# Hybrid attention layer on one core: weights' low parts between norm sums, and four subtractions on GpSimd

## The chip, the cores and the metric

The kernel runs on one core of a Trainium2 chip. The metric is the device time of one execution in microseconds, as the median of several executions. The engines are named as the profile names them: PE (TensorE's matrix multiplications), PEld (its weight loads), DVE (VectorE), ACT (ScalarE), POOL (GpSimd) and SP (SyncE, which here only issues DMAs).

## The reference

A layer with D = S = 1024, batch 1, depth 1, in float32. The input is normalised, multiplied by one wide weight matrix and split; differential softmax attention (8 heads) and gated linear attention (GLA, 4 heads) run on the parts; both are normalised, gated, joined, multiplied by `w_out`, normalised and added to the input.

```python
h = rms_norm(x, pre_g)                          # over D
z = einsum('bsd,de->bse', h, w_in)              # 1024 x 1024 x 7184
qa, ka, va, ga, qb, kb, vb, gb, gk_low = split_columns(z)
oa = diff_attention(qa, ka, va, lam)            # causal, two softmax maps a head
oa = rms_norm(oa, subln_g) * (1 - lam_init) * silu(ga)
log_a = log_sigmoid(gk_low @ w_gk_up + b_gk) / 16
ob = rms_norm(gla_chunked(qb, kb, vb, log_a), gla_g) * silu(gb)
x + rms_norm(concat([oa, ob]) @ w_out, post_g)
```

## The kernel before

**Products.** Each float32 operand of a large product is split into a high part, cast to the type that PE takes (ACT: `CAST`), and a low part, the operand less its high part (DVE: `TENSOR_TENSOR`). A product is three passes over PE: high by high, high by low, low by high. For `h @ w_in` both matrices are cut into 2 x 2 blocks and multiplied by a seven-product scheme (Strassen's, in Winograd's form): sums and differences of blocks are formed first, and seven products, numbered 1 to 7, take the place of eight. `LEFT` gives the left factor of each: `h11`, `h12`, `s4`, `h22`, `s1`, `s2`, `s3` for products 1 to 7.

**Steps.** `order` is a list of (column group, product). `go` walks it; `prepare` makes the weights of a step some steps ahead, `step` issues its matmuls. The first two column groups (`GATED`, the columns VB) come first, with products 1, 2, then 5, 6, 7, 4; `gated_weights(n)` makes their weights for both groups at once, two 128x1024 tiles `hi(0)`, `hi(1)` on ACT and two low parts `lo(0)`, `lo(1)` on DVE. For product 7 it leaves `lo` in the list `between`, from which the caller takes it.

**The first 80 us.** `norm_x` sums squares of a 128-row block of x (ACT), adds epsilon (DVE, `ssq`) and raises to -1/2 (POOL, `ssq`); `scale_x` multiplies the block's rows by it (DVE). `first(0)` and `first(1)` transpose rows 0 to 511 on PE (`xT`) and make `h11` and `h12` (`f1` keeps the unsplit `h12`); short `spin` products keep PE at work between the transposes. `blocks(j)` does so for rows 512 to 1023 (`t21`, `t22` and their sum `s1`); `differences(j)` makes s2 = t22 - (h11 - t21) in the tiles `s24` and splits it. Then follow `h22`, `s3` and, last, s4 = f1 - s2, which is written over s2 in `s24` by four DVE subtractions and then split.

**Product 6 to product 7.** Both add into the same PSUM banks, named x. Between them ACT copies a bank out (`COPY s<-x`), so the matmuls of product 7 of a column group may write only when the two copies of that group are done. Product 7 of the first group is the 24 matmuls that start near 66.5 us in the profile, that of the second the next 24.

**Order.** A scheduler orders the instructions of each engine's queue by a model of the time, within the dependences; instructions marked by `keep_in_program_order` (all while `pinned` holds) stay as written, and `tc.issue_after(i)` keeps what follows behind instruction i. Each engine then runs its queue strictly in that order, and waits on semaphores of the others.

**Helper lines.** Calls by way of `Queue` have line 66, matmuls line 144, transposes line 147; instructions are therefore told apart by their tiles. In names with buffer numbers (`s24_619`), the number is that of the tile.

Of the kernel before, what the change touches and what calls it, by code (L numbers as in the profile page):

```python
# [11 lines left out]
ALU = mybir.AluOpType  # L12
# [4 lines left out]
D = 1024  # L17
# [14 lines left out]
def hymba_kernel(  # L32
# [42 lines left out]
    act, dve, pool = Queue(nc.scalar), Queue(nc.vector), Queue(nc.gpsimd)  # L75

    def fp(t):
        return t.bitcast(F32)

    def cols(half):  # L80
        return slice(half * 512, half * 512 + 512)
# [239 lines left out]
    def gated_weights(n):  # L321

        name = {5: "b12"}.get(n)
        if name:
            load_gated(name)
        b11, b12, b21, b22, again = (
            gated_raws.get(name) for name in ("b11", "b12", "b21", "b22", "b21x")
        )
        src = {1: b11, 2: b21, 5: b11, 6: b11, 7: b12, 4: again, 3: b22}[n]
        a, b = {5: (b12, b11), 7: (b22, b12), 4: (again, b11)}.get(n, (None, None))  # L330
        own = {2: 1, 5: 1, 6: 3, 4: 1}.get(n)
        w = []
        for i in range(4):
            if i == own:
                w.append(kp.tile([P, 2, 512], F32R, tag="ks1", name="w"))
            elif n == 2 and i > 1:
                w.append(hw.tile([P, 2, 512], F32R, tag=f"h22_lo{i - 2}", name="w"))
            else:
                w.append(ap.tile([P, 2, 512], F32R, tag="ring", name="w", bufs=NRING))
        def hi(i):  # L340
            if a:
                dve.tensor_tensor(src[i], a[i], b[i], ALU.subtract)
            act.copy(w[i], src[i])

        def lo(i):
            lows[n] = dve.tensor_tensor(w[2 + i], src[i], fp(w[i]), ALU.subtract)

        if n == 1:
            for k in range(2):
                dve.tensor_copy(w[0][:, k], src[0][:, k])  # L350
            between[:] = [
                lambda: lo(1),
                lambda: (scale_x(3, cols(1)), lo(0)),
                lambda: act.copy(w[1][:, 1], src[1][:, 1]),
                lambda: (act.copy(w[1][:, 0], src[1][:, 0]), scale_x(2, cols(1))),
                lambda: [scale_x(st, cols(1)) for st in range(2)],
            ]
            return w[:2], w[2:]
        hi(0)
        if n == 7:  # L360
            hi(1)
            casts.append(act.latest)
            between.append(lo)
        else:
            hi(1)
            lo(0)
            lo(1)
        return w[:2], w[2:]

    between, lows = [], {}  # L370
# [181 lines left out]
    sums, key_stores, casts = {}, [], []  # L552
# [125 lines left out]
    def scale_x(st, cs):  # L678
        x_cs = xs[st][:, cs]
        return dve.tensor_scalar(x_cs, x_cs, norms[st], 1.0, ALU.mult, ALU.mult)  # L680
# [33 lines left out]
    for st in range(2):  # L714
        norm_x(st)
        scale_x(st, cols(0))
    norm_x(2)
    norm_x(3)
    scale_x(2, cols(0))
# [11 lines left out]
    f1 = hpool.tile([P, HB, 512], F32, tag="s4_lo0", name="f1")  # L731
# [26 lines left out]
    def parts(n, j, f, after=None):  # L758
        hi, lo = block(n)
        act.copy(at(hi, j), f)  # L760
        with tc.issue_after(after.ins) if after else nullcontext():
            return dve.tensor_tensor(at(lo, j), f, fp(at(hi, j)), ALU.subtract)
# [80 lines left out]
        prepare(i)  # L843
    first(0)
    norm_x(4, 5)
    for st in (4, 5):
        scale_x(st, slice(0, D))
    between.pop()()
    norm_x(6, 7)
    for st in (6, 7):  # L850
        scale_x(st, slice(0, D))
    hold[0] = 4
    for i in (2, 3):
        prepare(i)
# [14 lines left out]
    s24 = [kp.tile([P, 2, 512], F32, tag=f"k{i}", name="s24") for i in range(2)]  # L869
# [14 lines left out]
    for j in range(HB):  # L884
        s3_lo = parts("s3", j, t21[:, j], h22_lo)
# [5 lines left out]
    for i in range(2):  # L891
        for j in range(2 * i, 2 * i + 2):
            s = s24[i][:, j % 2]
            with tc.issue_after(s3_lo.ins):
                dve.tensor_tensor(s, f1[:, j], s, ALU.subtract)
        if not i:
            w_lo = between.pop()
            w_lo(0)
        for j in range(2 * i, 2 * i + 2):
            behind = [parts("s4", j, s24[i][:, j % 2], None if i else lows[7])]  # L900
        if not i:
            load_again(1)
            with tc.issue_after(behind[0].ins):
                w_lo(1)
# [365 lines left out]
    def parts_of(n):  # L1270
        return [(0, n)] if n <= 512 else [(0, 512), (512, n)]
# [27 lines left out]
    def scores(h, qb):  # L1299

        n = (qb + 1) * P
        qc = slice(qb % 4 * P, qb % 4 * P + P)
        st = const.tile([P, 6], F32, tag="stt", name="stt", bufs=4)
        if h == 0 and qb == NT - 1:
            for row, i in ((4, 7), (5, 6)):
                p1s[row] = pp.tile([P, (i + 1) * P], F32, tag=f"p0_{i}", name="p1", bufs=2)
        p0 = pp.tile([P, n], F32, tag=f"p0_{qb}", name="p0", bufs=1 + (qb > 5))
        if h == 0 and qb < 2:
            p1s[qb] = smp.tile([P, 512], F32, tag=("r", "fold")[qb], name="p1", bufs=1)
        p1 = p1s.pop(qb, None) or smp.tile([P, S], F32, tag="p1", name="p1", bufs=2)  # L1310
        for m, p in enumerate((p0, p1)):
            q = qk[h, "q", qb // 4][:, m, qc]
            parts = parts_of(n)
            if h == DA_HEADS - 1 and (qb, m) in ((1, 1), (0, 0), (0, 1)):

                parts = [(0, 512)]
            for i, (a, b) in enumerate(parts):
                sc = sc_bank("sc", [P, 512])
                for j, name in enumerate(("k", "ks")):
                    for half in range(2):  # L1320
                        lo, hi = max(a, half * 512), min(b, half * 512 + 512)
                        if lo < hi:
                            mm(
                                sc[:, lo - a : hi - a], q,
                                qk[h, name, half][:, m, lo - half * 512 : hi - half * 512],
                                start=(j == 0), stop=(j == 1),
                            )
                e = min(b, n)
                last = i == len(parts) - 1

                forced = (h, qb) == (0, NT - 2) or (h, qb, m) == (0, 3, 0)
                forced = forced or ((h, qb) == (0, 4) and m + i > 0)
                behind = tc.issue_after(lowest[0]) if forced else nullcontext()
                with behind:
                    ins = dve.tensor_tensor_reduce(
                        p[:, a:e], sc[:, : e - a],
                        maskt[:, NZ + P - (e - a) :] if last else maskt[:, : e - a],
                        1.0, 3e38 if i == 0 else st[:, 4 + m : 5 + m], ALU.add, ALU.min,
                        st[:, m : m + 1] if last else st[:, 4 + m : 5 + m],
                    )  # L1340
                if (h, qb) == (0, NT - 1):
                    lowest[:] = [ins.ins]
                c = 0.08 + (e - a) / 512 * 0.56
                if last:
                    act.activation(
                        p[:, :n], p[:, :n], AF.Exp, bias=st[:, m : m + 1], scale=-1.0,
                        accum_out=st[:, 2 + m : 3 + m],
                    )
                if last and m:
                    rec = dve.reciprocal(st[:, 4:6], st[:, 2:4])  # L1350
                    if h == 0 and qb in (4, 5):
                        lowest[:] = [rec.ins]
                    pool.tensor_scalar(
                        p1[:, :n], p1[:, :n], st[:, 5:6], lam, ALU.mult, ALU.mult
                    )
                    if qb != 5:
                        while mixed:
                            with tc.issue_after(ins.ins):
                                mixed.pop(0)()

                    def mix_maps():
                        dve.scalar_tensor_tensor(
                            p0[:, :n], p0[:, :n], st[:, 4:5], p1[:, :n], ALU.mult, ALU.subtract
                        )
                        w[h, qb] = p0

                    if h == 0 and qb > 2:
                        mixed.append(mix_maps)
                    else:
                        mix_maps()  # L1370
                    c += 0.25 + n / 1024 * 1.4
                yield c

    lowest, mixed, p1s = [], [], {}

    def all_scores():
        for h in range(DA_HEADS):
# [469 lines left out]
```

## Time and profile before

| | |
|---|---|
| median of 3 runs | 961.26 us (960.8 to 961.41) |
| the profiled execution | 960.34 us, its span 958.6 us |
| granted TensorE clock | 0.998 |
| busy | PE 948.2, PEld 793.2, DVE 742.3, ACT 604.7, POOL 193.9 us |

The span is the time from the first to the last instruction on the engines; the execution's own time is 1.7 us more. PE is busy for nearly all of it, but the other engines decide when it starts and whether it waits.

| us of the span | PE busy | DVE busy | ACT busy | POOL busy |
|---|---|---|---|---|
| 0 to 20 | 17.73 | 11.05 | 14.12 | 5.64 |
| 20 to 40 | 20.00 | 19.19 | 16.18 | 1.41 |
| 40 to 64 | 24.00 | 21.73 | 12.49 | 0.97 |
| 64 to 80 | 15.22 | 15.67 | 9.42 | 1.38 |

### The profile page before, as it was taken

How to read it: one execution, taken by the hardware profiler on the slowest of the kernel's cores; microseconds unless marked ns; L12 is line 12 of the kernel's file. 1: busy time of each engine (PE TensorE's matmuls, PEld its weight loads, DVE VectorE, ACT ScalarE, POOL GpSimd, SP SyncE). 2: the span in 40 equal slices, each digit the busy share in tenths (PEclk: the TensorE clock that was granted, in tenths of full speed). 3: DMA queues.
4: the chain of work that ended last, by engine and by line, in shares of the span. 5: the costliest groups of instructions: out<-in, count | busy, mean ns of one | idle time of the engine just before them, and what ended most of it. 6: DMA issues, size and time to landing. Idle time of an engine off the chain costs nothing.

```text
span 958.6 us, 14358 instructions
## 1 busy us (share of the span) xinstructions
PE 948.2 (99%) x4624; PEld 793.2 (83%) x4624; DVE 742.3 (77%) x1476; ACT 604.7 (63%) x1162; POOL 193.9 (20%) x263
## 2 busy tenths in 40 slices
PE   9999999999999999999999999999999999999997
PEld 7877788888888888888888888888888888888885
DVE  5998799996778787687767476588888888898464
ACT  7753355845777556577765444366677677787773
POOL 2001002222141112131100002122222222433321
PEclk9999999999999999999999999999999999999999
DMA  8546367487577897986755498996665679994776
GB/s 285 162 149 172 91 203 244 168 293 249 188 255 242 275 305 255 295 258 216 263 175 154 143 298 265 411 291 217 220 223 193 222 230 349 331 291 105 160 206 141
DMA packets 153258, 220.34 MB, mean 230 GB/s; under 512 B 15776, under 2 KB 85664, under 8 KB 153088
## 3 DMA queue, kind: packets, MB, share of 16 engines
q1 hardware_dynamic: 138736, 177.65, 57.8%
q0 software_dynamic: 14448, 41.79, 14.8%
q8 instruction: 36, 0.59, 0.3%
q14 instruction: 38, 0.31, 0.1%
HBM read 133.93 MB, written 88.60 MB: 232 GB/s over the span
## 4 chain that ended last, share of the span: by engine, by line
PE 96%; DVE 1%; ACT 1%; DMA 1%; issue 0%; POOL 0%; SPq 0%; DVEq 0%; ACTq 0%
PE x L144 23%; PE z L144 16%; PE y L144 16%; PE ypart L144 14%; PE sc L144 7%; PE po L144 5%; PE yps L144 4%; PE wtr L147 3%; PE gpo L144 3%; PE kv L144 1%; PE gkl_ps L144 1%; PE pa L144 1%; PE xT L147 1%; DMA x<-in_x_dram 1%; PE ms L144 0%; PE pk L147 0%
## 5 line engine op out<-in xcount | busy, mean ns | idle before, releaser
L66 ACT CAST w<-w_raw 128x512 fp32r<-128x512 f32 x138 | 85.1, 620 | 70.0 <-PE y L144 31.7
L66 ACT ACTIVATE p<-p,stt 128x896 f32<-128x896 f32 (+7 forms) x128 | 99.3, 777 | 30.8 <-DVE stt L66 29.9
L66 DVE TENSOR_TENSOR w<-w_raw,w 128x512 fp32r<-128x512 f32 x138 | 94.0, 684 | 31.5 <-ACT w L66 31.4
L66 ACT COPY s<-x 128x512 f32<-128x512 f32 x78 | 44.7, 584 | 65.1 <-PE x L144 64.9
L66 DVE CUSTOM_DVE_ANT_0 p<-sc,maskt 128x512 f32<-128x512 f32 (+3 forms) x128 | 74.2, 585 | 14.5 <-PE sc L144 13.2
L66 POOL TENSOR_SCALAR p<-p,stt,lam 128x1024 f32<-128x1024 f32 (+3 forms) x64 | 55.9, 874 | 143.9 <-DVE stt L66 143.8
L144 PE MATMUL z<-s_hi,w 128*128 128x512 f32 x320 | 80.1, 393 | 0.0
L144 PE MATMUL x<-s_hi,w 128*128 128x512 f32 x320 | 80.0, 392 | 0.0
L144 PE MATMUL y<-h_hi,w 128*128 128x512 f32 x320 | 80.0, 392 | 0.0
L144 PE MATMUL ypart<-wo_hi,m_hi 128*128 128x512 f32 x192 | 79.5, 414 | 0.1
L144 PE MATMUL ypart<-wo_hi,m_lo 128*128 128x512 f32 x192 | 75.5, 393 | 0.0
L144 PE MATMUL ypart<-wo_lo,m_hi 128*128 128x512 f32 x192 | 75.4, 393 | 0.0
L66 POOL DMA_DIRECT2D wo_d<-wo_hi x32 | 17.4, 543 | 270.4 <-ACT wo_hi L66 270.4
L144 PEld LDWEIGHTS z<-s_hi,w 128*128 128x128 f32 x320 | 59.8, 188 | 12.3
L144 PEld LDWEIGHTS x<-s_hi,w 128*128 128x128 f32 x320 | 59.7, 188 | 12.3
L144 PEld LDWEIGHTS y<-h_hi,w 128*128 128x128 f32 x320 | 59.7, 188 | 12.2
L144 PE MATMUL sc<-k,q 128*128 128x512 f32 (+1 forms) x192 | 68.9, 362 | 0.1
L144 PE MATMUL sc<-ks,q 128*128 128x512 f32 (+1 forms) x192 | 66.1, 347 | 0.0
L66 ACT CAST wt_hi<-wtr 128x512 fp32r<-128x512 f32 (+1 forms) x80 | 42.8, 534 | 29.0 <-PE wtr L147 28.3
L66 DVE TENSOR_TENSOR wt_lo<-wtr,wt_hi 128x512 fp32r<-128x512 f32 (+1 forms) x80 | 50.6, 633 | 9.9 <-ACT wt_hi L66 9.1
L66 DVE TENSOR_TENSOR w_raw<-w_raw 128x512 f32<-128x512 f32 x80 | 56.2, 703 | 1.4 <-DMA w_raw<-in_w_in_dram 0.4
L66 DVE TENSOR_TENSOR c<-z,s 128x512 f32<-128x512 f32 x48 | 32.8, 687 | 31.3 <-ACT s L66 19.3
(234 smaller groups left out, 2348.0 us busy)
## 6 DMA issues: line engine op xcount, KB each, us to landing
w_raw<-in_w_in_dram SPq DMA_DIRECT2D x40, 512.0 KB, 4.9
wo_d<-wo_hi POOLq DMA_DIRECT2D x32, 256.0 KB, 3.0
q<-q_d SPq DMA_DIRECT2D x32, 256.0 KB, 5.3
k<-k_d SPq DMA_DIRECT2D x32, 256.0 KB, 5.5
ks<-k_d SPq DMA_DIRECT2D x64, 128.0 KB, 6.2
wo_raw<-in_w_out_dram POOLq DMA_DIRECT2D x31, 256.0 KB, 5.0
v<-v_d SPq DMA_DIRECT2D x14, 512.0 KB, 7.7
wo_d<-gqd POOLq DMA_DIRECT2D x22, 256.0 KB, 4.1
```

What stands on the lines that cost most here:

```text
L66: ins = op(*a, **k)
L144: tc.keep_in_program_order(pe.matmul(*a, **k))
L147: tc.keep_in_program_order(pe.transpose(dst, src, ident))
```

## The change

```diff
                 lambda: (act.copy(w[1][:, 0], src[1][:, 0]), scale_x(2, cols(1))),
-                lambda: [scale_x(st, cols(1)) for st in range(2)],
+                lambda: scale_x(1, cols(1)),
...
             hi(1)
             lo(0)
+            if n == 2:
+                between.pop()()
             lo(1)
...
         norm_x(st)
         scale_x(st, cols(0))
+        if not st:
+            scale_x(st, cols(1))
...
     norm_x(4, 5)
+    between.pop()()
     for st in (4, 5):
         scale_x(st, slice(0, D))
-    between.pop()()
     norm_x(6, 7)
-    for st in (6, 7):
-        scale_x(st, slice(0, D))
+    between.append(lambda: [scale_x(st, slice(0, D)) for st in (6, 7)])
...
         for j in range(2 * i, 2 * i + 2):
             s = s24[i][:, j % 2]
-            with tc.issue_after(s3_lo.ins):
-                dve.tensor_tensor(s, f1[:, j], s, ALU.subtract)
+            pool.tensor_tensor(s, f1[:, j], s, ALU.subtract)
...
         for j in range(2 * i, 2 * i + 2):
-            behind = [parts("s4", j, s24[i][:, j % 2], None if i else lows[7])]
+            with tc.issue_after(casts[1]):
+                behind = [parts("s4", j, s24[i][:, j % 2], None if i else lows[7])]
...
-                with behind:
+                row = tc.issue_after(read[-1]) if h == 0 and qb == 5 and read else nullcontext()
+                with behind, row:
...
+                read[:] = [ins.ins]
```

The second half of the first 128 rows of x is scaled right behind its first half, ahead of the second row block's sum. The scalings of blocks 4 to 7 each get a low part of weights in front of them. The four subtractions of s4 are POOL's, no longer held behind s3, and the split of s4 stands behind the second weight cast of product 7 (`casts[1]`). The last edit, in the attention scores, holds an instruction behind the one issued before it; it leaves the order of all five queues as it was.

DVE's queue near the sums of blocks 4 to 7, before; `w_244` is the low part `lo(1)` of product 1, `w_326` and `w_327` those of product 2, `xt` the rows that are scaled:

```order
L66 TENSOR_TENSOR w_243<-g_raw_196,w_241 128x1024
L66 TENSOR_SCALAR ssq_305<-ssq_305 128x2
L66 TENSOR_SCALAR xt_201<-xt_201,ssq_305 128x1024
L66 TENSOR_SCALAR xt_203<-xt_203,ssq_305 128x1024
L66 TENSOR_TENSOR w_244<-g_raw_197,w_242 128x1024
L66 TENSOR_SCALAR ssq_315<-ssq_315 128x2
L66 TENSOR_SCALAR xt_205<-xt_205,ssq_315 128x1024
L66 TENSOR_SCALAR xt_207<-xt_207,ssq_315 128x1024
L66 TENSOR_TENSOR w_326<-g_raw_194,w_324 128x1024
L66 TENSOR_TENSOR w_327<-g_raw_195,w_325 128x1024
```

The same place in the changed kernel (its `w_245` is `w_244` above, its `w_324` and `w_325` are `w_326` and `w_327`):

```order
L66 TENSOR_TENSOR w_244<-g_raw_196,w_242 128x1024
L66 TENSOR_SCALAR ssq_305<-ssq_305 128x2
L66 TENSOR_TENSOR w_245<-g_raw_197,w_243 128x1024
L66 TENSOR_SCALAR xt_201<-xt_201,ssq_305 128x1024
L66 TENSOR_SCALAR xt_203<-xt_203,ssq_305 128x1024
L66 TENSOR_SCALAR ssq_315<-ssq_315 128x2
L66 TENSOR_TENSOR w_324<-g_raw_194,w_322 128x1024
L66 TENSOR_SCALAR xt_205<-xt_205,ssq_315 128x1024
L66 TENSOR_SCALAR xt_207<-xt_207,ssq_315 128x1024
L66 TENSOR_TENSOR w_325<-g_raw_195,w_323 128x1024
```

One low part has moved between each pair's `ssq` and its scalings, where POOL's power lies.

ACT's queue between product 6 and product 7, before; `w_735`, `w_736` are the high parts of product 7's weights, `s_823`, `s_825` the two copies of the second group's x banks, `s4_hi` the casts of s4, and the last two rows the copies after product 7 of the first group:

```order
L66 CAST w_735<-g_raw_498 128x1024
L66 CAST w_736<-g_raw_499 128x1024
L66 COPY s_823<-x_334 128x512
L66 COPY s_825<-x_335 128x512
L66 CAST s4_hi_746<-s24_619 128x512 x2
L66 CAST s4_hi_746<-s24_620 128x512 x2
L66 COPY g_raw_498<-x_332 128x512
L66 COPY g_raw_498<-x_333 128x512
```

The same in the changed kernel:

```order
L66 CAST w_735<-g_raw_498 128x1024
L66 CAST w_736<-g_raw_499 128x1024
L66 CAST s4_hi_746<-s24_619 128x512 x2
L66 CAST s4_hi_746<-s24_620 128x512 x2
L66 COPY s_823<-x_334 128x512
L66 COPY s_825<-x_335 128x512
L66 COPY g_raw_498<-x_332 128x512
L66 COPY g_raw_498<-x_333 128x512
```

The two copies have moved behind the four casts of s4, each of which needs one of the four subtractions.

POOL's queue in the changed kernel from the last powers on; before, the two rows with `s24` are not there:

```order
L66 TENSOR_TENSOR ssq_305<-ssq_305,eps_t_76 128x2
L66 TENSOR_TENSOR ssq_315<-ssq_315,eps_t_76 128x2
L66 DMA gk_up_912<-in_w_gk_up_dram 16x512
L66 DMA wd_914<-in_w_in_dram 128x8x16
L66 TENSOR_TENSOR s24_619<-f1_241,s24_619 128x512 x2
L66 TENSOR_TENSOR s24_620<-f1_241,s24_620 128x512 x2
L66 MEMSET gkl_907 128x1024
L66 MEMSET wl2_909 128x768
```

Four instructions with two SBUF inputs each have come into POOL's queue; their rows on DVE, between the differences of product 7's weights and the low part `w_737`, are gone.

More of the change, by code (lines that the diff above doesn't have):

```diff
@@ L1372, in scores @@
                 yield c
-    lowest, mixed, p1s = [], [], {}
+    lowest, mixed, read, p1s = [], [], [], {}
     def all_scores():
```

## The prediction

> **What bounds the kernel.** I read the page first: the busy times and the chain that ended last. Then what PE waited for, the first 80 us engine by engine, and, since work goes to POOL, every place where POOL and DVE run together.
>
> ```profile
> PE 948.2 (99%) x4624; PEld 793.2 (83%) x4624; DVE 742.3 (77%) x1476; ACT 604.7 (63%) x1162; POOL 193.9 (20%) x263
> PE 96%; DVE 1%; ACT 1%; DMA 1%; issue 0%; POOL 0%; SPq 0%; DVEq 0%; ACTq 0%
> PE spin L144 <- POOL idle L66: 1.5, 1, 1.5
> PE x L144 <- DVE w L66: 0.8, 1, 0.8
> PE xT L147 <- DVE x L66: 0.7, 1, 0.7
> ```
>
> PE is the chain, and only three waits of it show, 3.0 us in all, the first ahead of anything that changes. So the change cannot bring much; it is worth what it does to the other two, and it can cost what it makes PE wait anew. The wait on `w` is the one to look at:
>
> ```profile
> 64.73 3.82 PE L144 MATMUL x<-w,s_hi 128*128 128x512 f32 x16
> 70.23 1.07 PE L144 MATMUL x<-w,s_hi 128*128 128x512 f32 x4
> 72.07 3.02 PE L144 MATMUL x<-w,s_hi 128*128 128x512 f32 x12 [0.78 <-DVE w L66]
> 74.93 1.98 PE L144 MATMUL x<-w,s_lo 128*128 128x512 f32 x8
> 76.74 1.98 PE L144 MATMUL x<-w,s_hi 128*128 128x512 f32 x8
> ```
> ```profile
> 63.78 2.35 DVE L66 TENSOR_TENSOR g_raw<-g_raw 128x1024 f32<-128x1024 f32 x2
> 66.05 2.49 DVE L66 TENSOR_TENSOR s<-f,s 128x512 f32<-128x512 f32 x4
> 68.46 1.22 DVE L66 TENSOR_TENSOR w<-g_raw,w 128x1024 fp32r<-128x1024 f32 x1
> 69.60 1.28 DVE L66 TENSOR_TENSOR s_lo<-s,s_hi 128x512 fp32r<-128x512 f32 x2
> 70.80 1.21 DVE L66 TENSOR_TENSOR w<-g_raw,w 128x1024 fp32r<-128x1024 f32 x1
> ```
>
> Eight matmuls go from 74.93 to 76.74: 0.226 each. Product 7 of the first group therefore starts at 64.73 + 8 x 0.226 = 66.54. Its last four matmuls could follow at 70.23 + 4 x 0.226 = 71.13; they start at 72.07, when the second low part of its weights (70.80 + 1.21) is there. PE loses 0.94. DVE is late because the four subtractions `s<-f,s` stand ahead of both low parts and DVE has no gap from 61.37 on.
>
> **The parts, and what each costs.**
>
> *The scaling moved forward at the start.* Its 0.4 on DVE (two took 0.87 at 12.72) now delays the second block's sum, so the second transposes come at 8.45 to 8.5 instead of 8.05. Behind them PE runs spins and then waits for the third block, which hangs on its load:
>
> ```profile
> 8.05 0.64 PE L147 MATMUL xT<-ident,x 128*128 128x128 f32 x4
> 8.45 1.41 PE L144 MATMUL spin<-idle,ones 128*128 128x512 f32 x5
> 10.53 1.23 PE L147 MATMUL xT<-ident,x 128*128 128x128 f32 x8 [0.68 <-DVE x L66]
> 12.72 0.87 DVE L66 TENSOR_SCALAR x<-x,ssq 128x512 f32<-128x512 f32 x2
> 7.61 1.06 ACT L66 ACTIVATE junk<-x 128x1024 f32<-128x1024 f32 x1 [0.99 <-DMA x<-in_x_dram]
> ```
>
> The spins end near 10.3 instead of 9.86, still before 10.53. Cost nothing, cover 0.2; without it, the delay less 0.2. The third wait of PE stays.
>
> *Low parts between sums and scalings.* DVE waits 0.81 twice for POOL's power:
>
> ```profile
> 17.65 0.70 POOL L66 TENSOR_TENSOR ssq<-ssq,eps_t 128x2 f32<-128x2 f32 x1 [7.14 <-DVE ssq L66]
> 18.38 1.42 DVE L66 TENSOR_SCALAR xt<-xt,ssq 128x1024 f32<-128x1024 f32 x2 [0.81 <-POOL ssq L66]
> 8.87 0.68 DVE L66 CUSTOM_DVE_ANT_0 junk<-x 128x512 f32<-128x512 f32 x1
> L66 POOL TENSOR_TENSOR ssq<-ssq,eps_t x6: 564/640/924, 5.6 to 21.1; 128x1 f32<-128x1 f32 x4, 128x2 f32<-128x2 f32 x2
> ```
>
> A low part (1.21) in each wait would gain up to 1.6. But the longest of the six powers, 924 against a median of 640, is the one beside `junk`, a DVE instruction with two SBUF inputs: POOL seems to be held out by such an instruction, and a low part is one. Then the power ends 0.4 behind the low part and the gain shrinks to some 0.7, plus the 0.4 of the scaling that left the middle. I take 1.1, between 0 and 2.0. It does not reach PE by itself: DVE soon waits for transposes that PE paces.
>
> *Order of DVE from 40 to 56.* The changed order puts `c<-y,s` and the last two `s_lo` where the waits before (0.60 at 44.99, 0.69 at 55.26) mostly vanish:
>
> ```profile
> 44.99 0.69 DVE L66 TENSOR_TENSOR c<-y,s 128x512 f32<-128x512 f32 x1 [0.60 <-PE y L144]
> 55.26 0.69 DVE L66 TENSOR_TENSOR s_lo<-s,s_hi 128x512 fp32r<-128x512 f32 x1 [0.69 <-ACT s_hi L66]
> 55.86 2.35 DVE L66 TENSOR_TENSOR w<-g_raw,w 128x1024 fp32r<-128x1024 f32 x2
> 61.37 2.50 DVE L66 TENSOR_TENSOR s_lo<-t,s_hi 128x512 fp32r<-128x512 f32 x4 [0.74 <-ACT s_hi L66]
> ```
>
> 55.86 - 0.60 - 0.69 = 54.6; with what is left of the first gain I take 54.2 for the two `w`.
>
> *The subtractions on POOL.* On DVE four take 2.4 (66.05 to 68.46). POOL's nearest row is `gate`, two SBUF inputs of the same shape:
>
> ```profile
> L66 POOL TENSOR_TENSOR gate<-r,gate 128x512 f32<-128x512 f32 x14 | 18.5, 1320 | 41.1 <-DVE r L66 31.2 <-DVE stt L66 9.9
> L66 POOL TENSOR_SCALAR_AFFINE_SELECT gan<-gan x8: 647/1566/6864, 233.7 to 489.0; 128x512 f32<-128x512 f32 x8
> 271.10 6.86 POOL L66 TENSOR_SCALAR_AFFINE_SELECT gan<-gan 128x512 f32<-128x512 f32 x1
> 271.36 0.69 DVE L66 TENSOR_TENSOR w<-w_raw,w 128x512 fp32r<-128x512 f32 x1
> ...
> 276.78 0.69 DVE L66 TENSOR_TENSOR w<-w_raw,w 128x512 fp32r<-128x512 f32 x1
> ```
> ```profile
> 344.51 0.86 POOL L66 TENSOR_SCALAR_AFFINE_SELECT gan<-gan 128x512 f32<-128x512 f32 x1
> 344.79 1.12 DVE L66 TENSOR_TENSOR go<-go,gg 128x512 fp32r<-128x512 f32 x1
> ```
>
> So 1.30 each where nothing is in the way, 5.2 for four; they may start once s2 is split (51 to 54 us) and are needed from 66 on. That looks ample. But the selects say otherwise: one shape, 0.65 to 6.86 us. The long one lies beside ten DVE instructions with two SBUF inputs, back to back, and ends 0.5 behind the last; the DVE instructions keep their 0.69. The short one at 344.51 got in after one instruction, and then DVE's took 1.12 instead of 0.69. So the two take turns, DVE without a gap keeps POOL out, and POOL once in holds DVE for about its own length: 1.30 less some 0.15 of start, 1.15 (bounds 0.9 and 1.3).
>
> The Trainium skill says it as a rule ("SBUF — State Buffer", section "Who interferes with whom"): a DVE instruction with two SBUF inputs contends with a GpSimd instruction that reads SBUF, and whichever issues first holds the pair for its whole length. It speaks against this move, and the selects agree with the holding; taken as strict turns by issue, it would let POOL in after one DVE instruction each time, which is a rival below.
>
> Where DVE pauses, with everything in the place that the order gives it:
>
> 1. The pause ahead of the last `s_lo` (some 0.17 left): the first subtraction, 53.4 to 54.6; the two `w` start at 54.2 + 1.15 - 0.17 = 55.2.
> 2. Two `w` and four `h_lo` last 55.86 to 60.62 before, so they end at 59.9; in the 0.74 pause for `s_hi` the second goes in, and the four `s_lo` start at 61.0 instead of 61.37. The first difference of product 7's weights follows 2.41 later (63.78 - 61.37), at 63.4, ends at 64.65, and its cast (1.05, as at 74.39) at 65.7: in time for 66.54.
> 3. The first low part waits for that cast; the third subtraction takes the pause, 65.7 to 66.85. The second low part follows 1.14 + 2 x 0.60 later, at 69.2, and ends at 70.4: 0.7 before 71.13. **PE's wait is gone, -0.94.**
> 4. DVE runs on without a pause to 70.9. Only then does the fourth subtraction get in, 70.9 to 72.1. The fourth cast `s_hi` on ACT waits for it, and in ACT's new order the two copies of the second group stand behind that cast:
>
> ```profile
> 67.12 1.06 ACT L66 COPY s<-x 128x512 f32<-128x512 f32 x2
> 68.07 2.19 ACT L66 CAST s_hi<-s 128x512 fp32r<-128x512 f32 x4
> 74.39 1.05 ACT L66 CAST w<-g_raw 128x1024 fp32r<-128x1024 f32 x1 [0.24 <-DVE g_raw L66]
> 78.44 0.95 POOL L66 MEMSET gkl<- 128x1024 f32 x1 [33.37 <-DVE w L66]
> ```
>
> Before, the copies ended at 68.2. Now the cast starts at 72.1, the copies 0.52 later (2.19 is three such steps and a last cast of 0.63) and end at 73.2 and 73.7. Product 7 of the second group would start at 66.54 + 24 x 0.226 = 71.97 and needs both for its first two matmuls: 73.7 + 0.1 - 0.23 = 73.55. **A new wait, +1.55** (0.5 with 0.9 a hold, 2.1 with 1.3).
>
> Behind that the queues have room: the fourth `s_lo` comes at 72.8, then a difference (1.22) and the first weight cast of product 4 (1.05, by 75.7 with ACT's copies ahead of it), needed at 73.55 + 24 x 0.226 = 79.0; POOL's memsets, at 78.44 before, stand behind subtractions that end at 72.1; POOL's two DMAs are ahead of them, and SP's order is unchanged. Sum: -0.94 + 1.55 = +0.6. The traced execution took 960.34 (span 958.6 and 1.7 around it) and would take 960.95; it is 0.92 below the median of 961.26, so the median becomes 961.9.
>
> **Rivals.**
>
> *It works.* The subtractions slip in early enough, as the select at 344.51 did, or POOL's two-input instruction is not held out as a select is. The fourth must end by 70.3 (71.97 less a cast of 0.63 and copies to 0.06 behind it). Then -0.94 stands alone: 960.3. For: a slip between two DVE instructions is enough, and there are six from 66.9 on. Against: the select at 271.10, and that the median of the eight is 1.57, not 0.65.
>
> *Strict turns.* POOL gets in after each DVE instruction as soon as s2 is split: four holds of 1.15 at 51.6 to 60, only 0.2 of them in pauses. The first weight difference comes at 54.2 + 4.6 + 7.9 = 66.7 instead of 62.1, its cast ends near 69.0, 2.5 behind 66.54; nothing waits after it. 2.5 to 3.3 instead of 0.94: slower by 1.6 to 2.4, 963.2. It decides from the second hold outside a pause on, since 2.1 us lie between that cast unheld (64.4) and 66.54.
>
> *Nothing moves.* The gain at `w` and a short wait for the copies cancel, 961.2; this lies inside the forecast's bounds and is counted with it.
>
> **How the numbers follow.** The forecast (960.8 to 962.4 by the bounds of a hold) gets 0.47, "it works" 0.32 (960.0 to 960.7), strict turns 0.16 (962.7 to 963.8), something else 0.05. From 960.0 to 963.2 some 0.2 is left out, half of it with the strict turns. A measurement here tells about 0.2%, 1.9 us: faster than 959.3 only by something unforeseen (0.03); slower than 963.2 by half the strict turns and a little (0.10); else the same.
>
> **What would show it.** Right: no wait of PE on `w` near 72, a wait on `s` of ACT in its place, a `s<-f,s` row on POOL of several us, the copies near 73. Wrong: four POOL rows of 1.3 before 60; `w` on DVE starting before 66.5 with the copies before 71.9 (it works); or PE waiting on ACT's `w` at 66.5 (strict turns).

## The result, and the profile after

The changed kernel takes 963.69 us (median of nine runs, 962.6 to 964.77), the kernel before 960.73 beside it: ratio 1.0029, 95% interval 1.0019 to 1.0039. It is slower by 0.3%; the interval leaves out 1, so the loss is small but clear of the noise. The forecast was 961.9, 0.6 above the 961.26 that the kernel before had then, and between 960.0 and 963.2 with its rivals; the measured median is 3.0 above the kernel before beside it. The profiled execution took 962.6 with a span of 960.9, against 960.34 and 958.6 before.

The page of the changed kernel (busy times; chain that ended last) and its list of PE's waits:

```profile
PE 948.9 (99%) x4624; PEld 792.7 (83%) x4624; DVE 744.9 (78%) x1472; ACT 604.6 (63%) x1162; POOL 205.2 (21%) x267
PE 92%; DVE 4%; ACT 2%; DMA 1%; issue 1%; POOL 0%; SPq 0%; DVEq 0%; ACTq 0%
PE x L144 <- ACT w L66: 2.0, 1, 2.0
PE spin L144 <- POOL idle L66: 1.5, 1, 1.5
PE xT L147 <- DVE x L66: 0.7, 1, 0.7
```

PE's wait on DVE's `w` is gone, as wanted. A longer one, on ACT's `w`, has come four microseconds sooner (from 67.40 instead of 71.30). The timeline of that place, PE first and then POOL, DVE and ACT, and below it the four `h_lo` of the kernel before:

```profile
65.42 1.98 PE L144 MATMUL x<-w,s_hi 128*128 128x512 f32 x8
69.37 2.33 PE L144 MATMUL x<-w,s_hi 128*128 128x512 f32 x8 [1.98 <-ACT w L66]
51.95 9.56 POOL L66 TENSOR_TENSOR s<-f,s 128x512 f32<-128x512 f32 x4 [7.90 <-DVE s_lo L66]
53.52 2.38 DVE L66 TENSOR_TENSOR s_lo<-s,s_hi 128x512 fp32r<-128x512 f32 x2
55.82 4.54 DVE L66 TENSOR_TENSOR w<-g_raw,w 128x1024 fp32r<-128x1024 f32 x2
60.28 3.58 DVE L66 TENSOR_TENSOR h_lo<-t,h_hi 128x512 fp32r<-128x512 f32 x4
67.02 2.35 DVE L66 TENSOR_TENSOR g_raw<-g_raw 128x1024 f32<-128x1024 f32 x2
68.27 2.18 ACT L66 CAST w<-g_raw 128x1024 fp32r<-128x1024 f32 x2 [1.17 <-DVE g_raw L66]
```
```profile
58.14 2.49 DVE L66 TENSOR_TENSOR h_lo<-t,h_hi 128x512 fp32r<-128x512 f32 x4
```

Read the first from the bottom. Product 7's weights are cast at 68.27 because DVE comes to their differences only at 67.02 (63.78 before). DVE is late because its two `w` take 4.54 us instead of 2.35 and its four `h_lo` 3.58 instead of 2.49: exactly beside POOL's four subtractions, which take 9.56 us instead of the 5.2 that four would take alone. PE is idle for 1.98 there and for 0.37 more in the middle of the product, where the second cast is due: 2.35 in all. From start to start, the measure that gave 0.94 before, it loses a little more: ready at 65.42 + 8 x 0.226 = 67.23, it goes on at 69.37, 2.14 later, and with 0.36 in the middle that is 2.5.

Two other places changed. PE's `y` product near 32 us, and the norm section:

```profile
31.50 1.03 PE L147 MATMUL xT<-ident,xt 128*128 128x128 f32 x8
32.67 2.11 PE L144 MATMUL y<-w,h_hi 128*128 128x512 f32 x8
31.93 0.68 DVE L66 TENSOR_TENSOR gv_st<-y,s 128x512 f32<-128x512 f32 x1
17.53 1.60 POOL L66 TENSOR_TENSOR ssq<-ssq,eps_t 128x2 f32<-128x2 f32 x1 [6.75 <-DVE ssq L66]
19.17 1.41 DVE L66 TENSOR_SCALAR xt<-xt,ssq 128x1024 f32<-128x1024 f32 x2 [0.59 <-POOL ssq L66]
24.84 2.49 DVE L66 TENSOR_TENSOR h_lo<-f,h_hi 128x512 fp32r<-128x512 f32 x4
```

From the transposes to the `y` product it is 1.17 us instead of 0.79 (31.23 to 32.02 before): the product waits for its bank, which `gv_st` empties, and `gv_st` now stands behind one more weight difference and a `t` (31.93 instead of 30.77).

The span grew by 2.3: 0.27 at the start (the third transposes come at 10.80 instead of 10.53), 0.38 at the `y` bank, 1.4 at product 7, and some 0.2 spread behind. (The product behind product 7 starts at 80.61 instead of 78.55, 2.06 later, and 0.65 of that was there before.)

### The profile page after: what moved, and what is told of

It reads as the page before. It is cut to its first block, busy times and chain, and to the rows that moved or that the text cites. A ratio compares the mean times of both kernels' runs of the same rounds, so it can differ in the third digit from the quotient of the medians.

```text
span 960.9 us, 14362 instructions
## 1 busy us (share of the span) xinstructions
PE 948.9 (99%) x4624; PEld 792.7 (83%) x4624; DVE 744.9 (78%) x1472; ACT 604.6 (63%) x1162; POOL 205.2 (21%) x267
## 4 chain that ended last, share of the span: by engine, by line
PE 92%; DVE 4%; ACT 2%; DMA 1%; issue 1%; POOL 0%; SPq 0%; DVEq 0%; ACTq 0%
PE x L144 22%; PE y L144 15%; PE z L144 15%; PE ypart L144 13%; PE sc L144 7%; PE po L144 5%; PE yps L144 4%; PE wtr L147 3%; PE gpo L144 3%; PE kv L144 1%; DVE p L66 1%; PE gkl_ps L144 1%; PE pa L144 1%; DVE w L66 1%; DMA x<-in_x_dram 1%; DVE s_lo L66 1%
## 5 line engine op out<-in xcount | busy, mean ns | idle before, releaser
L66 POOL TENSOR_SCALAR p<-p,stt,lam 128x1024 f32<-128x1024 f32 (+3 forms) x64 | 55.9, 874 | 144.5 <-DVE stt L66 141.3
```

The source lines that it names most:

```text
L66: ins = op(*a, **k)
```

## The experiments

The theory: POOL and DVE hold each other out, one turn each, and the holds make product 7's weights late. Rivals: the reordered norm section costs the time; DVE is late because it depends on POOL's results.

**1. The subtractions back on DVE, all else as changed** (the split of s4 is no longer held behind `casts[1]` either).

```
-            pool.tensor_tensor(s, f1[:, j], s, ALU.subtract)
+            with tc.issue_after(s3_lo.ins):
+                dve.tensor_tensor(s, f1[:, j], s, ALU.subtract)
```

> The changed kernel with the four fourth-difference subtractions back on DVE; low parts between the norm sums, the early scaling and the rest stay. If POOL's subtractions cost the time (they hold DVE out for 1.1 us each): the rows `w` and `h_lo` on DVE between 54 and 64 us are back at 1.21 and 0.62 us an instruction, no wait of PE on ACT's `w` near 67; the 0.4 us wait near 32 us for the y bank stays; DVE reaches product 7's low parts about 1 us sooner than in the kernel before, so most of its 0.94 us wait goes: 960.0 to 960.7, level with before. If the re-ordered norm section costs the time: about 963.5, as the changed kernel.

960.22 (959.8 to 960.48), 0.9994 of before (0.9985 to 1.0003). Timeline of DVE and PE:

```profile
55.07 2.35 DVE L66 TENSOR_TENSOR w<-g_raw,w 128x1024 fp32r<-128x1024 f32 x2
62.99 2.35 DVE L66 TENSOR_TENSOR g_raw<-g_raw 128x1024 f32<-128x1024 f32 x2
65.58 3.79 PE L144 MATMUL x<-w,s_hi 128*128 128x512 f32 x16
69.21 1.98 PE L144 MATMUL x<-w,s_lo 128*128 128x512 f32 x8
71.02 3.79 PE L144 MATMUL x<-w,s_hi 128*128 128x512 f32 x16
```

DVE is 0.8 ahead of before, and PE runs through product 7 in both groups without a wait. So the other edits take the wait of 0.94 away by themselves. The 0.35 near 32 us stayed (31.66 to 32.80), and the start was 0.4 late.

**2. The kernel before with only the subtractions moved.** (The edit is the reverse of that, with the change's `issue_after(casts[1])`, and its `row` edit, which keeps the order of later work.)

> The kernel before with only the four subtractions moved to POOL. If they cost the time: POOL gets in at the pause of DVE near 54.6 to 55.3 us and then takes turns with it, three or four holds of about 1.1 us, PE waits 2 to 2.7 us on ACT's `w` near 67, the 0.94 us wait near 72 is gone, no wait near 32: 962.0 to 962.7. If the norm section costs the time: 959.8 to 960.7.

964.8 (963.25 to 965.31), 1.0038 (1.0026 to 1.0051): the loss is POOL's, and the norm section is cleared of it, but for the `y` bank: with the old norm section nothing is lost there (31.55 to 32.34). It was more than expected:

```profile
56.51 4.54 DVE L66 TENSOR_TENSOR w<-g_raw,w 128x1024 fp32r<-128x1024 f32 x2
70.06 3.66 PE L144 MATMUL x<-w,s_hi 128*128 128x512 f32 x8 [2.31 <-ACT w L66]
73.56 2.00 PE L144 MATMUL x<-w,s_lo 128*128 128x512 f32 x8
```

The wait is 2.31 as foretold, but the eight matmuls behind it take 3.66 us instead of 1.98: the granted clock between 69 and 74 us is 0.66 on average. PE also loses 0.43 on product 6's last low part, the second of the `w` in the first row. More on this in experiments 5 and 9.

**3. Four POOL subtractions whose results nothing reads**, added to the first experiment. Behind 100 us DVE, ACT and POOL run in that kernel's order, the attention stage too, so its whole time can be read, though of one run only.

```
+    scrap = maskt[:, :NZ]
+    for j in range(HB):
+        pool.tensor_tensor(scrap, f1[:, j], s24[j // 2][:, j % 2], ALU.subtract)
+    pool.memset(scrap, 0.0)
```

> The first of these kernels (subtractions on DVE) plus four POOL subtractions of the same operands at the same place, whose results nothing reads (they go to the mask tile, zeroed again behind them). Only the stretch from 40 to 80 us is to be read: later work of the attention stage stands in another order. If the two engines hold each other out: POOL's first row is long (3 us or more), the DVE rows `w` and `h_lo` beside it go to 2.3 and 1.8 us an instruction, DVE loses 4 to 4.5 us, though no DVE instruction waits for POOL. If DVE was late because it depended on POOL's results: all DVE rows keep 0.62 to 1.22 us.

964.39. POOL's rows and the DVE rows beside them:

```profile
48.54 3.36 POOL L66 TENSOR_TENSOR maskt<-f,s 128x512 f32<-128x512 f32 x2
56.67 1.63 POOL L66 TENSOR_TENSOR maskt<-f,s 128x512 f32<-128x512 f32 x1 [4.77 <-DVE s L66]
48.93 1.80 DVE L66 TENSOR_TENSOR t<-h_lo,t 128x512 f32<-128x512 f32 x1
50.65 3.47 DVE L66 TENSOR_TENSOR g_raw<-g_raw 128x1024 f32<-128x1024 f32 x2
56.45 2.40 DVE L66 TENSOR_TENSOR s_lo<-s,s_hi 128x512 fp32r<-128x512 f32 x2
```

These twins could start some microseconds sooner, so other DVE rows carry the holds: 1.80 instead of 0.68 and 3.47 instead of 2.35 are 1.12 each. Product 7's differences come at 66.68 instead of 62.99, and PE waits 1.22 and 0.89. No DVE instruction here reads what POOL wrote: it is the two engines' meeting that costs, not a dependence.

**4. Dose: two subtractions on POOL, two on DVE.**

```
+            if i:  # the last two
+                with tc.issue_after(s3_lo.ins):
+                    dve.tensor_tensor(s, f1[:, j], s, ALU.subtract)
+            else:
                 pool.tensor_tensor(s, f1[:, j], s, ALU.subtract)
```

> The changed kernel with only the first two subtractions on POOL, the last two back on DVE ahead of product 7's low parts. If each subtraction on POOL holds DVE out for 1.1 us: DVE reaches product 7's weight differences 2.2 us later than with none on POOL (62.99), at about 65.2; the cast on ACT then ends at 67.4, when PE is there; the second low part is some 0.4 us late: PE waits 0.3 to 0.8 us in all, 960.4 to 961.1, and the granted clock does not fall. If any use of POOL there costs the whole wait: 962.5 or more.

960.31 (959.57 to 961.42), 0.9998 (0.9989 to 1.0007).

```profile
55.73 3.44 DVE L66 TENSOR_TENSOR w<-g_raw,w 128x1024 fp32r<-128x1024 f32 x2
64.73 2.35 DVE L66 TENSOR_TENSOR g_raw<-g_raw 128x1024 f32<-128x1024 f32 x2
65.31 4.12 PE L144 MATMUL x<-w,s_hi 128*128 128x512 f32 x16
```

One `w` is held (3.44 = 2.35 + 1.09) and one `s_lo`. The differences come at 64.73, 1.74 behind the first experiment's, and PE loses 0.3 within the 16 matmuls: two holds just use up the slack, four overdraw it.

**5. Dose: six on POOL.**

```
             pool.tensor_tensor(s, f1[:, j], s, ALU.subtract)
+            if not i:
+                pool.tensor_tensor(s, s, maskt[:, :NZ], ALU.add)
```

> The changed kernel with six instructions of two SBUF inputs on POOL instead of four: the first two subtractions each get a second one behind them that adds the zeros of the mask tile. If each holds DVE out for 1.1 us: PE's wait on ACT's `w` near 67 us grows from 2.35 to about 4.5 us. If a wait of PE beyond some 2.5 us also makes the granted clock fall behind it (matmuls of 0.43 instead of 0.23 us for 3 us): all runs lie together, at 966.0 to 966.8. If the wait alone counts: 964.6 to 965.1, and as spread as the changed kernel's runs.

966.82 (965.8 to 967.23), 1.0065 (1.0052 to 1.0077). The timeline of PE, and PE's busy time and granted clock (the number behind the count) in two stretches:

```profile
71.34 3.22 PE L144 MATMUL x<-w,s_hi 128*128 128x512 f32 x8 [4.18 <-ACT w L66]
74.36 2.67 PE L144 MATMUL x<-w,s_lo 128*128 128x512 f32 x8
69.00:74.00 5.00, 2.66 (x8) 0.84 0.00 0
74.00:80.00 6.00, 6.00 (x24) 0.85 0.45 118
```

All five runs lie high, with a granted clock of 0.994 to 0.997 over the whole execution. The wait grew from 1.98 to 4.18, 1.1 for each of the two instructions added. From its end to the last eight matmuls of the first group (71.34 to 76.87) it takes 5.53 us, where the changed kernel's first profile has 3.99 (69.37 to 73.36): 1.54 more. Together that is 3.7 of the 4.6 us by which this execution's span (965.5) exceeds that one's (960.9).

**6. POOL copies with one input instead of the twins**, in the loop of experiment 3.

```
+        pool.tensor_copy(scrap, s24[j // 2][:, j % 2])
```

> As the idle twins, with a copy (one SBUF input) in place of each of POOL's four subtractions, results again unread. If one input on POOL's side is enough for the two engines to hold each other out: DVE rows beside the copies are longer by a copy's length less about 0.2 us, and POOL's copies are held up. If it takes two inputs on both sides: DVE's rows keep 0.68 and 1.21 us and four copies end within a few us.

960.93.

```profile
46.42 3.23 POOL L66 COPY maskt<-s 128x512 f32<-128x512 f32 x3 [2.53 <-DVE s L66]
48.08 1.10 DVE L66 TENSOR_TENSOR t<-h_lo,t 128x512 f32<-128x512 f32 x1
49.10 2.76 DVE L66 TENSOR_TENSOR g_raw<-g_raw 128x1024 f32<-128x1024 f32 x2
```

One SBUF input on POOL's side is enough. But the hold is short: 1.10 - 0.68 = 0.42 and 2.76 - 2.35 = 0.41, where a subtraction holds 1.1.

**7. Is it the arrival? The four subtractions made to come one by one**, by dependences on product 6's last low part, the last `h_lo` and the last `s_lo`.

```
+            made_by = pool.tensor_tensor(s, f1[:, j], s, ALU.subtract).ins
+            gate = (None, lows[6].ins, h22_lo.ins, s3_lo.ins)[j]
+            ...
```

> The changed kernel with POOL's four subtractions made to arrive one by one: the second behind product 6's last low part, the third behind the last `h_lo`, the fourth behind the last `s_lo` near 63 us. If a POOL instruction that arrives while DVE runs without a gap is kept out, and only one that follows another POOL instruction takes its turn: the second one's row is some 3.5 us long and ends in DVE's pause near 61 us, the four `h_lo` beside it keep 2.5 us in all, the third takes one turn among the `s_lo`. If POOL gets in after each DVE instruction in any case: the second one's row is 1.7 us and the four `h_lo` take 3.6 us. Either way fewer holds lie ahead of product 7's weight differences than in the changed kernel: they start 1 to 2 us sooner than its 67.02, PE waits 0.3 to 1.3 instead of 2.35 us, 960.6 to 961.8, and the granted clock stays full.

962.48 (961.49 to 963.18), 1.0013 (1.0004 to 1.0022).

```profile
52.31 3.40 POOL L66 TENSOR_TENSOR s<-f,s 128x512 f32<-128x512 f32 x1 [7.91 <-DVE s_lo L66]
58.68 1.60 POOL L66 TENSOR_TENSOR s<-f,s 128x512 f32<-128x512 f32 x1 [2.97 <-DVE w L66]
65.91 2.20 POOL L66 TENSOR_TENSOR s<-f,s 128x512 f32<-128x512 f32 x1 [2.43 <-DVE s_lo L66]
58.45 3.58 DVE L66 TENSOR_TENSOR h_lo<-t,h_hi 128x512 fp32r<-128x512 f32 x4
65.75 3.44 DVE L66 TENSOR_TENSOR g_raw<-g_raw 128x1024 f32<-128x1024 f32 x2
70.32 1.21 PE L144 MATMUL x<-w,s_hi 128*128 128x512 f32 x4 [1.03 <-ACT w L66]
```

A subtraction that comes upon DVE running without a gap (58.68, 65.91) gets in after the instruction that is under way. No earlier POOL instruction is needed for that. The time missed the expectation: the last one held the second difference of product 7's weights itself (3.44), and its cast kept PE 1.03.

**8. Is it POOL's idle time ahead of the first?** Wherever POOL does these subtractions, the row of the first lasts 3.4 us (2.8 in experiment 2). A small fill of `maskt` puts POOL to work just before:

```
+        pool.memset(maskt[:, :64], 0.0)   # waits for the last g_raw difference ahead
```

> The changed kernel with a small fill of the mask tile with the zeros that it holds already (128x64) put on POOL behind DVE's last instruction ahead of the `s_lo` of s2 (near 51 us), so that POOL comes to the first subtraction at once instead of after 7.9 us without work. If that idle time is why the first subtraction lies idle through three or four DVE instructions: its row shortens from 3.4 to under 2 us and the hold begins 1.5 us sooner. If the DVE instructions there keep it out: the row stays at 3.4 us.

964.34, and the first row does not change: single records show 3.397 us with 0.54 of idle time ahead of it, and 3.397 with 7.90 in the changed kernel.

```profile
51.14 0.15 POOL L66 MEMSET maskt<- 128x64 f32 x1 [7.21 <-DVE g_raw L66]
51.83 9.56 POOL L66 TENSOR_TENSOR s<-f,s 128x512 f32<-128x512 f32 x4 [0.54 <-DVE s_lo L66]
```

So POOL's idle time is not the reason. The first subtraction is kept out through DVE's `c`, `s` and `s_lo` there until a gap, as the long select of the prediction was. Why it is kept out there and not among `h_lo`, `w` and `g_raw` stays open.

**9. The changed kernel again, for its two groups of runs.**

> The changed kernel once more, for one profile. Its runs lay in two groups, 962.6 to 963.0 and 963.7 to 964.8 us. If the upper group is the fall of the granted clock behind PE's wait near 67 us: a run of that group shows the eight matmuls behind the wait at 0.43 instead of 0.23 us and a granted clock under 0.9 between 69 and 74 us; a run of the lower group shows neither.

963.16, with the matmuls behind the wait at 2.35 for eight and a clock of 1.00.

> The changed kernel a third time, for one profile; the profile so far was of the lower group of runs. If this run lies at 963.7 us or above, the eight matmuls behind PE's wait near 67 us are longer than 0.3 us each and the granted clock between 69 and 74 us is under 0.95; if it lies below, neither is.

964.24, and this is the other group:

```profile
69.51 3.40 PE L144 MATMUL x<-w,s_hi 128*128 128x512 f32 x8 [1.98 <-ACT w L66]
72.70 2.33 PE L144 MATMUL x<-w,s_lo 128*128 128x512 f32 x8
74.87 3.79 PE L144 MATMUL x<-w,s_hi 128*128 128x512 f32 x16
69.00:74.00 5.00, 4.49 (x13) 0.66 0.09 10
```

The same wait of 1.98, but from its end to the last eight matmuls of the first group (69.51 to 74.87) it takes 5.36 us, in the first profile 3.99 (69.37 to 73.36). The 1.37 between them is most of what parts the groups (span 962.4 against 960.9). In this trace the clock stands at 0.50 from 69.98 to 73.39. The nine runs of the result say the same: over the whole execution the granted clock was 0.998 to 0.999 in the four of the lower group and 0.996 to 0.997 in the five of the upper one.

**10. Two ways to do without POOL.** First, the kernel before with both low parts of product 7 ahead of the four subtractions:

```
+    w_lo = between.pop()
+    w_lo(0)
+    w_lo(1)
     for i in range(2):
         ...  # the subtractions, now behind the second low part, and parts("s4", ...)
```

> The kernel before with both low parts of product 7's weights put ahead of the four subtractions on DVE, nothing else moved to another engine. If PE's 0.94 us wait is only DVE's order there: low parts at 66.1 and 67.3 us, no wait of PE near 72, 959.8 (0.999 of before). If the casts and low parts of the fourth differences, now 2.4 us later, are needed at once, a wait on `s` takes its place: 960.7 or more.

960.88 (960.03 to 961.6), 1.0002 (0.9993 to 1.0011).

```profile
70.31 3.79 PE L144 MATMUL x<-w,s_hi 128*128 128x512 f32 x16
79.66 0.72 PE L144 MATMUL y<-w,h_hi 128*128 128x512 f32 x2 [1.03 <-ACT w L66]
76.22 1.23 DVE L66 TENSOR_TENSOR g_raw<-g_raw 128x1024 f32<-128x1024 f32 x1
```

The 0.94 is gone and comes back as 1.03 one product on: the scheduler now sets two `gv_st` ahead of product 4's second weight difference (76.22 instead of 74.82), and its cast on ACT falls behind two copies.

Then the first experiment with the eviction near 31 us put first:

```
-                dve.tensor_tensor(src[i], a[i], b[i], ALU.subtract)
+                with tc.issue_after(evicted[0]) if (n, i) == (5, 1) else nullcontext():
+                    dve.tensor_tensor(src[i], a[i], b[i], ALU.subtract)
```

> The first experiment (subtractions on DVE) with the second weight difference of product 5 put behind the first `gv_st` near 31 us. If the 0.35 us that PE loses near 32 us hangs on that eviction of the y bank, it goes: 959.6 to 960.0, the fastest so far. If PE waits there for something else: 960.2 as before.

959.65 (959.15 to 960.87), 0.9993 (0.9984 to 1.0002).

```profile
31.39 1.03 PE L147 MATMUL xT<-ident,xt 128*128 128x128 f32 x8
32.19 2.07 PE L144 MATMUL y<-w,h_hi 128*128 128x512 f32 x8
```

0.80 from transposes to product, as before the change: PE's loss there hung on the eviction. In the time the gain doesn't show. The ratio is that of the first experiment (0.9994), and the profiled execution (960.32) has a new wait of 0.5 on DVE's `c` near 145 us, one that experiment 5 shows too (0.4). Each held against the kernel before beside it, this kernel and the first experiment's lie some 3.4 us below the changed one; from the kernel before they can't be told apart.

## Why the prediction came out as it did

- **What bounds the kernel**: right as far as it went. Only waits of PE moved the time, but the clock that falls behind one of them was not in the sum.
- **The scaling moved forward at the start**: right, nothing. The third transposes hang on the load of `x`: they came at 10.81 in experiment 2, which has the old order, and at 10.80 in the changed kernel.
- **Low parts between sums and scalings**: the price was right, the neighbourhood not looked at. The power was held out as foreseen (1.60 instead of 0.70), and DVE's wait left 0.59 of 0.81; `h_lo` comes 0.59 sooner (24.84, 25.43 before) although the start is 0.27 later: a gain of 0.86, against 1.1. But "it does not reach PE by itself" was wrong: with these edits the order near 30 us is another, the first `gv_st` went behind, and PE lost 0.38 (experiment 2, without them, loses nothing there). Only the waits between 40 and 56 us had been followed through the new order.
- **Order of DVE from 40 to 56**: right on the waits, too early by 0.9. The two waits were to vanish: `c<-y,s` has none left, the last `s_lo` 0.2 (experiment 1). But the two `w` came at 55.07 there, not at 54.2, because PE, which paces DVE, was itself some 0.75 later (start and `y` bank).
- **The hold on DVE**: right. 1.15 was taken, 1.09 to 1.12 measured (0.92 for the first, part of which lay in a pause of DVE).
- **When POOL gets in**: this step failed. "DVE without a gap keeps POOL out" was drawn from one select that lay through ten DVE instructions, and the four subtractions were placed by it in DVE's pauses. Item 1 came true (the first subtraction waited for the gap near 54.2). Item 2 did not: the second was to wait for the pause at 60, and went in at 55.9, ahead of the first `w`; all four were done at 61.5, not 72.1. So all four stood ahead of product 7's weight differences, not two, and these came at 67.02, not at 63.4. PE did not wait for the copies `s<-x` (72.44), and the +1.55 of the sum did not come; in its place came 2.35 us of waiting for product 7's casts, which had been placed in time (65.7 for 66.54). The Trainium skill's rule ("SBUF — State Buffer", section "Who interferes with whom"), that whichever of the two issues first holds the pair for its whole instruction, was read in the prediction as one turn each and set below the select. Three of the four turns of the changed kernel agree with that reading; the first, which three DVE instructions keep waiting, does not.
- **The rival "strict turns"** had the place and nearly the wait: 2.5 behind 66.54 was foreseen, 2.14 behind 67.23 measured. It had the time of the runs with the full clock: 1.6 to 2.4 above the kernel before was foreseen, and the lower group's median, 962.7, is 2.0 above 960.73. It lacked the clock: the upper group lies 1.6 higher still, and as five of the nine runs are in it, so does the median. That 963.2 is near the median of 963.69 is in part luck.
- **The wait on `w` that was to go** did go, and experiment 1 shows that the norm edits alone were enough for it: the move to POOL bought nothing that was still for sale.

## What to carry to other kernels

Before work is moved to POOL to relieve DVE, count what each of its instructions will hold DVE: here 1.1 us for a subtraction of 128x512 that cost DVE itself 0.6. Where DVE is the late one, the move makes it later, even if POOL has nothing else to do and nobody waits for the result. And when an edit makes an engine come sooner, follow the new order as far as it differs, evictions of banks above all: the one that went behind cost 0.38 here, and a single ordering edge gave it back there.

## What the hardware showed that was not expected

- A wait of PE of about 2 us can cost nearly as much again. Behind 1.98 us without matmuls the clock fell in some runs of the same kernel and not in others (eight matmuls in 3.40 or 2.33 us); behind 4.18 us all five runs lie high, and the profiled one lost 1.5 us more on the matmuls than the changed kernel with the full clock. Where it fell, the traces have the clock at 0.50 for 3.41 us: from 69.98 us in the third profile of the changed kernel, from 70.04, 72.39 and 70.80 in experiments 2, 5 and 8.
- What decides between the two groups seems to be where the wait lies in a free-running stretch of 3.41 us. All four falls come 64.85 us, 19 times 3.413, behind the first record of the full clock (5.12 us in the third profile, where the `spin` matmuls go from 0.43 to 0.23 us apart). Cut into stretches from there, PE was idle for 1.98, 2.29, 2.37 and 1.87 us of the stretch just ahead of the fall. In the two profiles of the changed kernel with the full clock the same wait lies across the edge of two stretches, with 1.65 and 1.41 us in the longer part; 1.82 us, in an earlier stretch of experiment 5, brought no fall either. This is worked out from these traces; no run moved the wait on purpose. The Trainium skill ("TensorE: Matmul & The Clock Gate", Part 1) speaks of half the clock after an idle window of some 3.4 us that runs freely. The half and the free-running window agree with these traces, but here a gap of 2.4 us between weight loads was enough.
- A POOL instruction with one SBUF input also holds DVE, for 0.41 us at 128x512, one with two for 1.1. Beside `c<-y,s`, one of whose inputs lies in PSUM, DVE seems not to be held: the first twin came there, `c<-y,s` kept its 0.68, and the instruction behind it took 1.21 instead of 0.68, half a hold.
- The same two engines show both manners, one turn each and kept out until a gap. What decides it is open; idle time of POOL does not (experiment 8), nor a POOL instruction just ahead (experiment 7).
